# Weight sums in another order and a chunk ahead, the last gate behind the next chunk's first copy, and ScalarE and VectorE pinned to the written order in these chunks

## The chip, the core and the metric

The kernel runs on one core of a Trainium2 chip. The core has a matrix engine (TensorE), which writes its results to PSUM banks, a vector engine (VectorE), a scalar engine (ScalarE), GpSimd, and a sync engine that issues transfers. Each engine takes the instructions of its own queue one after the other and waits for the others through semaphores. The metric is the time of one execution on the device in microseconds; lower is better.

## What is computed

A stack of four layers over 256 tokens of width 1024, in float32. Each layer is a feed-forward block, an attention, and a second feed-forward block, each between norms and with a residual:

```python
def swiglu(x, w_in, w_out):
    gate, up = jnp.split(x @ w_in, 2, axis=-1)
    return (jax.nn.silu(gate) * up) @ w_out

for i in range(DEPTH):                       # DEPTH = 4
    h = h + 0.5 * rms_norm(swiglu(rms_norm(h, g[0]), ffn_w_in[i, 0], ffn_w_out[i, 0]), g[1])
    m = rms_norm(h, g[2])
    ...                                      # one of three kinds of attention
    h = h + rms_norm(m, g[3])
    h = h + 0.5 * rms_norm(swiglu(rms_norm(h, g[4]), ffn_w_in[i, 1], ffn_w_out[i, 1]), g[5])
```

The change touches the eight feed-forward blocks alone. A block's `w_in` is 1024 x 5632 (gate and up side by side), its `w_out` 2816 x 1024.

## The kernel before

**Products in three matmuls.** Every float32 weight is split into a high and a low part (`hilo`, lines 155 to 157): ScalarE copies the raw weights rounded to `hi` (line 156), VectorE subtracts `hi` from the raw ones to get `lo` (line 157). A product takes hi times hi, lo times hi and hi times lo, so three matmuls for each 128 rows of weights (`product`, line 152). A unit of weights is 128 partitions x 2048 elements, and its product on one token tile of 128 tokens is 12 matmuls of 512 columns.

**Chunks.** A block walks over the 2816 columns in six chunks: chunk 0 of 512, chunk 1 of 256, chunks 2 to 5 of 512. Chunks 0 and 1 go the plain way (`plain`). Chunks 2 to 5 (`WINO`) use a Winograd form of the 2 x 2 product of token tiles by gate and up: seven products instead of eight, of sums of the weights' four quarters. The quarters are b00 and b01 (upper half of the rows, gate and up) and b10 and b11 (lower half). Seven weight units come of them: b00, b10, t2 = b00 + b01 + b11, t1 = b00 + b01, t3 = b01 + b11, b11, and t4 = t2 + b10.

**How the sums are made before.** `plan_wino` (lines 359 to 400) splits b00, then VectorE adds b01 into b00's buffer (line 372, this is t1); it splits b10, then VectorE adds b00's buffer (now t1) and b11 into a fifth buffer, t2 (line 372 again), and GpSimd issues a transfer that adds b11 into b01's buffer (line 375, this is t3); it splits t2, then GpSimd adds b10 into t2's buffer (line 375, this is t4). So a chunk has two sums on VectorE and two accumulating transfers.

**One chunk on TensorE** (`wino`, lines 470 to 522). Bank B (tile `pb`) takes the product of b00; ScalarE copies it out as `sl0` (line 487). The gated result of the chunk before is turned (tile `tpg`, line 434) and split into `gh` and `gl`. Bank A (`pa`) takes b10; VectorE adds it to `sl0` (line 482, a small operation), ScalarE takes Silu (line 493). B takes t2 on top, and is copied out as `sl1` (line 498); then come the output products of the chunk before with its first `w_out` unit, o0, token tile 0 and then 1 (tile `y`, lines 244 to 246); B takes t1 on top and is copied out as `g1` (line 504); bank C (`pc`) takes t3, VectorE adds it to `g1` (line 482); B takes b11 on top, and VectorE makes the gated result of tile 0, `g` (`up`, line 426); output products with the second `w_out` unit, o2; C takes t4 on top. The last gate, of tile 1: VectorE adds C to `sl1` (line 482), ScalarE takes Silu (line 518), VectorE multiplies (line 426).

**What sets the order.** The code is handed to a scheduling pass, which orders each engine's queue by its own estimate of when operands are ready; the written order decides only where that pass sees a tie or a dependence. Weight units live in four buffers (`UNITS`): a split has to wait until TensorE is done with the unit that had the buffer before. Raw weights live in nine (`RAWS`). `fill` issues the next loads and splits as buffers are free.

## Time and profile before

| | |
|---|---|
| time, median of 3 runs | 2004.0 us (2003.55 to 2004.16) |
| profiled execution | 2004.23 us, of which the span of the instructions is 2002.3 us |
| TensorE busy | 1932.5 us, 97% of the span |
| VectorE busy | 1609.4 us, 80% |
| ScalarE busy | 1257.2 us, 63% |
| mean granted TensorE clock | 0.998 of full speed |

Busy time of TensorE is time in which at least one matmul is under way; matmuls overlap, so the idle time that the profile lists for it is only what is left between the end of one and the start of the next. A wait is written as the waiting instruction, an arrow, and the instruction that ended last among those it waited for.

### The profile page before, as it was taken

The page shows a single profiled execution, that of the slowest core. Times are in us where ns is not written, and L with a number is a line of the kernel's source. Part 1 is how long each engine was busy: PE and PEld are TensorE (multiplying, and loading weights), DVE is VectorE, ACT ScalarE, POOL GpSimd, SP SyncE. Part 2 cuts the span into 40 slices and gives each one's busy share as a digit, 9 for nine tenths or more (in the row PEclk, how much of TensorE's full clock was granted, in tenths as well). Part 3 has the DMA queues.
Part 4 walks back from the last instruction along what each step waited for, and adds up shares of the span by engine and source line. Part 5 has one row for each costly group of instructions (what it writes and reads, how often), then busy time and mean ns, then how long its engine had stood idle before and what let it go on. Part 6 is the DMA issues. An engine that isn't in the chain of part 4 may idle for free.

```text
span 2002.3 us, 25733 instructions
## 1 busy us (share of the span) xinstructions
PE 1932.5 (97%) x9712; PEld 1584.9 (79%) x9712; DVE 1609.4 (80%) x2040; ACT 1257.2 (63%) x1721; POOL 188.6 (9%) x303
## 2 busy tenths in 40 slices
PE   7999999999999999999999999999999999999998
PEld 6777878777877878877887787678778777878776
DVE  6888678888788766788879877877988888678886
ACT  6566666566566566566656666865666657576654
POOL 0001210000000120000000032000000000210000
PEclk9999999999999999999999999999999999999999
DMA  9795638696787556687877675166868785638782
GB/s 360 213 295 140 211 120 294 184 294 188 245 274 222 169 189 212 184 278 211 283 221 212 209 205 165 60 242 200 230 208 300 202 286 148 206 105 286 203 286 55
DMA packets 177867, 430.25 MB, mean 215 GB/s; under 512 B 8784, under 2 KB 37712, under 8 KB 169552
## 3 DMA queue, kind: packets, MB, share of 16 engines
q1 hardware_dynamic: 168528, 361.51, 50.7%
q0 software_dynamic: 9216, 67.11, 17.6%
q8 instruction: 76, 1.25, 0.2%
q14 instruction: 47, 0.39, 0.1%
HBM read 360.43 MB, written 1.05 MB: 181 GB/s over the span
## 4 chain that ended last, share of the span: by engine, by line
PE 79%; ACT 8%; DVE 7%; issue 3%; POOL 0%; ACTq 0%; DVEq 0%; POOLq 0%
PE ps L152 13%; PE pb L152 12%; PE y L246 9%; PE y L244 9%; PE y L245 9%; PE pc L152 6%; ACT hi L156 5%; PE pa L152 4%; PE pw L670 4%; PE pw L672 4%; PE pw L671 3%; DVE lo L157 3%; DVE raw L372 2%; PE tpg L434 1%; ACT gh L156 1%
## 5 line engine op out<-in xcount | busy, mean ns | idle before, releaser
L157 DVE TENSOR_TENSOR lo<-raw,hi 128x2048 fp32r<-128x2048 f32 (+3 forms) x534 | 984.7, 1861 | 251.3 <-ACT hi L156 250.8
L156 ACT CAST hi<-raw 128x2048 fp32r<-128x2048 f32 (+3 forms) x534 | 824.8, 1563 | 481.6 <-DVE raw L372 189.9
L244 PE MATMUL y<-hi,gh 128*128 128x512 f32 x704 | 277.6, 394 | 5.1 <-ACT gh L156 5.1
L245 PE MATMUL y<-lo,gh 128*128 128x512 f32 x704 | 275.2, 391 | 0.0
L246 PE MATMUL y<-hi,gl 128*128 128x512 f32 x704 | 265.7, 391 | 0.0
L152 PE MATMUL ps<-hi,xh 128*128 128x256 f32 (+1 forms) x512 | 175.4, 342 | 1.9 <-ACT xh L156 1.3
L152 PE MATMUL pb<-hi,sh 128*128 128x512 f32 x384 | 153.1, 399 | 21.1 <-ACT sl L487 21.1
L152 PE MATMUL ps<-lo,xh 128*128 128x256 f32 (+1 forms) x512 | 173.2, 338 | 0.2 <-DVE lo L157 0.2
L152 PE MATMUL ps<-hi,xl 128*128 128x256 f32 (+1 forms) x512 | 172.9, 338 | 0.0
L244 PEld LDWEIGHTS y<-hi,gh 128*128 128x128 f32 x704 | 132.2, 188 | 41.7 <-ACT gh L156 15.2
L670 PE MATMUL pw<-hi,xh 128*128 128x512 f32 (+2 forms) x432 | 164.6, 381 | 0.0
L672 PE MATMUL pw<-hi,xl 128*128 128x512 f32 (+2 forms) x432 | 155.9, 361 | 0.0
L671 PE MATMUL pw<-lo,xh 128*128 128x512 f32 (+2 forms) x432 | 155.4, 360 | 0.0
L246 PEld LDWEIGHTS y<-hi,gl 128*128 128x128 f32 x704 | 132.2, 188 | 27.4
L375 POOL DMA_DIRECT2D raw<-raw x64 | 55.5, 868 | 1037.6 <-DVE raw L372 644.3
L245 PEld LDWEIGHTS y<-lo,gh 128*128 128x128 f32 x704 | 132.3, 188 | 26.0
L152 PE MATMUL pb<-lo,sh 128*128 128x512 f32 x384 | 151.8, 395 | 0.0
L152 PE MATMUL pb<-hi,sl 128*128 128x512 f32 x384 | 149.5, 389 | 0.0
L372 DVE TENSOR_TENSOR raw<-raw,raw 128x2048 f32<-128x2048 f32 x64 | 146.0, 2282 | 0.0
L152 PEld LDWEIGHTS ps<-hi,xh 128*128 128x128 f32 x512 | 97.6, 191 | 13.2 <-ACT xh L156 2.2
L152 PEld LDWEIGHTS pb<-hi,sh 128*128 128x128 f32 x384 | 72.0, 188 | 45.3 <-ACT sl L487 31.2
L152 PEld LDWEIGHTS ps<-lo,xh 128*128 128x128 f32 x512 | 97.6, 191 | 11.2 <-DVE lo L157 1.1
(213 smaller groups left out, 3327.2 us busy)
## 6 DMA issues: line engine op xcount, KB each, us to landing
raw<-in_ffn_w_in SPq DMA_DIRECT2D x172, 1024.0 KB, 8.4
raw<-in_ffn_w_out SPq DMA_DIRECT2D x88, 1024.0 KB, 9.2
raw<-raw POOLq DMA_DIRECT2D x64, 1024.0 KB, 7.0
raw<-in_diff_w_in SPq DMA_DIRECT2D x24, 1024.0 KB, 5.2
raw<-in_moba_w_in SPq DMA_DIRECT2D x12, 1024.0 KB, 5.2
raw<-in_nsa_w_in SPq DMA_DIRECT2D x9, 1024.0 KB, 5.1
raw<-in_diff_w_out SPq DMA_DIRECT2D x8, 1024.0 KB, 4.9
gpre<-in_norm_g SPq DMA_DIRECT2D x12, 512.0 KB, 5.9
```

What stands on the lines that cost most here:

```text
L152: nc.tensor.matmul(out, l, r, start=first and i == 0, stop=last and i == len(steps) - 1, skip_group_check=more)
L156: self.nc.scalar.copy(hi, src)
L157: self.nc.vector.tensor_tensor(lo, src, hi.bitcast(F32), op=ALU.subtract)
L244: nc.tensor.matmul(y[b], x[0][:, kt, :], hi[:, k, s], start=f, stop=False)
L245: nc.tensor.matmul(y[b], x[0][:, kt, :], lo[:, k, s], start=False, stop=False)
L246: nc.tensor.matmul(y[b], x[1][:, kt, :], hi[:, k, s], start=False, stop=l)
L372: nc.vector.tensor_tensor(R[name(to)], R[name(a)], R[name(b)], op=ALU.add)
L375: nc.gpsimd.dma_start(R[name(to)], R[name(b)], accum_op=ALU.add)
L434: nc.tensor.transpose(tp[:, k, :], g[:, k * P:(k + 1) * P], self.ident)
L670: nc.tensor.matmul(out, x[0][:, kt, :], hi[:, k, :], start=first and i == 0, stop=False)
L671: nc.tensor.matmul(out, x[0][:, kt, :], lo[:, k, :], start=False, stop=False)
L672: nc.tensor.matmul(out, x[1][:, kt, :], hi[:, k, :], start=False, stop=last and i == len(todo) - 1)
```

## The change

Three things change in the Winograd chunks, none in the arithmetic of a product.

- **Sums.** A new `sums_of(j)` makes t1 = b00 + b01 on VectorE into the fifth buffer, and has GpSimd add b11 into b01 (t3). It is called one chunk ahead: in chunk j - 1 between the output products with o0 and the product of t1, and for chunk 2 in the plain chunk 1. When chunk j's units are prepared, b00 and b10 are split, and VectorE adds b01, which by then holds t3, into b00: that is t2. So the second sum now reads what the first transfer has written. After the split of t2, GpSimd adds b10 into b00's buffer (t4).
- **Last gate.** The three instructions of tile 1's last gate become `gate1`, which the next chunk calls right behind its copy of `sl0`; the last one is called after the loop.
- **Order.** While `wino` runs, `ordered` is set, and every split, copy, Silu, sum and small operation on ScalarE and VectorE that goes through `placed` is tied behind the instruction written before it on its engine. The scheduling pass no longer moves them.

The diff, cut to its core:

```diff
     def hilo(self, src, hi, lo):
-        self.nc.scalar.copy(hi, src)
-        self.nc.vector.tensor_tensor(lo, src, hi.bitcast(F32), op=ALU.subtract)
+        self.placed(self.nc.scalar.copy(hi, src))
+        self.placed(self.nc.vector.tensor_tensor(lo, src, hi.bitcast(F32), op=ALU.subtract))
+
+    def placed(self, ins):
+
+        return self.tc.keep_in_program_order(ins) if self.ordered else ins
...
-                               (name("b10"), quarter(1, 0)), (name("b11"), quarter(1, 1)), (name("t2"), None), *ko):
+                for n, src in ((name("b00"), quarter(0, 0)), (name("b01"), quarter(0, 1)), (name("b11"), quarter(1, 1)),
+                               (name("t1"), None), (name("b10"), quarter(1, 0)), *ko):
...
+                def sum_t2():
+                    split(name("b10"), name("b10"))
+                    self.placed(nc.vector.tensor_tensor(R[name("b00")], R[name("b00")], R[name("b01")], op=ALU.add))
+
+                def split_t2():
+                    split(name("t2"), name("b00"))
+                    nc.gpsimd.dma_start(R[name("b00")], R[name("b10")], accum_op=ALU.add)
...
-                    lambda: quarters("b00", [("b00", "b00", "b01")]),
-                    lambda: quarters("b10", [("t2", "b00", "b11"), ("b01", "b11")]),
-                    lambda: quarters("t2", [("t2", "b10")]),
+                    lambda: split(name("b00"), name("b00")),
+                    sum_t2,
+                    split_t2,
...
+            def sums_of(j):
...
+                while (j, "t1") not in R:
+                    loads.pop(0)()
+                b01 = R[j, "b01"]
+                self.placed(nc.vector.tensor_tensor(R[j, "t1"], R[j, "b00"], b01, op=ALU.add))
+                nc.gpsimd.dma_start(b01, R[j, "b11"], accum_op=ALU.add)
...
-            def wino(j):
+            def wino(j, gate1):
...
-                nc.scalar.copy(sl0, B)
+                place(nc.scalar.copy(sl0, B))
+                gate1()
...
                 o(1, 0)
+                sums_of(j + 1)
                 times(B, s31, 4, "t1", False)
...
-                add(sl1, C)
-                nc.scalar.activation(sl1, sl1, AF.Silu, scale=X[1][1])
-                up(1, g1, 512, sl1, j, nr[1], g1)
-                fill()
+
+                def gate1():
+                    add(sl1, C)
+                    place(nc.scalar.activation(sl1, sl1, AF.Silu, scale=X[1][1]))
+                    up(1, g1, 512, sl1, j, nr[1], g1)
...
-                    wino(j)
+                    self.ordered = True
+                    gate1 = wino(j, gate1)
+                    self.ordered = False
...
-                plain(j, zig, [lambda: turn(j - 1, 0), lambda: turn(j - 1, 1)])
+                plain(j, zig, [lambda: turn(j - 1, 0), lambda: turn(j - 1, 1), lambda: sums_of(j + 1)])
```

What it does to the queues is shown at the seam from chunk 3 to chunk 4 of layer 0's second block. Names: `pb`, `pa`, `pc` are the banks, `g01_3_1` the gated result of chunk 3, tile 1.

VectorE before. lo439 is o2 of chunk 2, lo441 t4 of chunk 3, lo445, lo446 and lo447 are b00, b10 and t2 of chunk 4, lo448 is o0 of chunk 3; raw423, raw424 and raw433 are b00, b01 and b11 of chunk 4, raw436 its t2:

```order
L157 TENSOR_TENSOR lo439_3537<-raw421_3320,hi439_3536 128x2048
L482 TENSOR_TENSOR g01_3_1_3554<-pc444_3564,g01_3_1_3554 128x512
L157 TENSOR_TENSOR lo441_3557<-raw416_3266,hi441_3556 128x2048
L157 TENSOR_TENSOR lo445_3579<-raw423_3350,hi445_3578 128x2048
L426 SCALAR_TENSOR_TENSOR g01_3_0_3595<-pb431_3433,st396_3004,sl01_3_0_3446 128x512
L372 TENSOR_TENSOR raw423_3350<-raw423_3350,raw424_3352 128x2048
L157 TENSOR_TENSOR lo446_3598<-raw430_3431,hi446_3597 128x2048
L372 TENSOR_TENSOR raw436_3482<-raw423_3350,raw433_3452 128x2048
L482 TENSOR_TENSOR sl01_3_1_3504<-pc444_3564,sl01_3_1_3504 128x512
L157 TENSOR_TENSOR lo447_3628<-raw436_3482,hi447_3627 128x2048
L426 SCALAR_TENSOR_TENSOR g01_3_1_3554<-g01_3_1_3554,st397_3006,sl01_3_1_3504 128x512
L157 TENSOR_TENSOR lo448_3648<-raw438_3510,hi448_3647 128x2048
```

VectorE after, the same stretch; raw433 is now t1 of chunk 4, lo449 is o0 of chunk 3:

```order
L158 TENSOR_TENSOR lo439_3537<-raw421_3320,hi439_3536 128x2048
L411 TENSOR_TENSOR raw433_3452<-raw423_3350,raw424_3352 128x2048
L158 TENSOR_TENSOR lo441_3559<-raw395_2990,hi441_3558 128x2048
L497 TENSOR_TENSOR g01_3_1_3556<-pc444_3566,g01_3_1_3556 128x512
L158 TENSOR_TENSOR lo445_3581<-raw423_3350,hi445_3580 128x2048
L439 SCALAR_TENSOR_TENSOR g01_3_0_3596<-pb429_3424,st396_3004,sl01_3_0_3437 128x512
L158 TENSOR_TENSOR lo446_3599<-raw436_3481,hi446_3598 128x2048
L379 TENSOR_TENSOR raw423_3350<-raw423_3350,raw424_3352 128x2048
L158 TENSOR_TENSOR lo447_3628<-raw423_3350,hi447_3627 128x2048
L497 TENSOR_TENSOR sl01_3_1_3504<-pc444_3566,sl01_3_1_3504 128x512
L439 SCALAR_TENSOR_TENSOR g01_3_1_3556<-g01_3_1_3556,st397_3006,sl01_3_1_3504 128x512
L158 TENSOR_TENSOR lo449_3663<-raw438_3510,hi449_3662 128x2048
```

The first sum moved five places forward, behind lo of o2; the small operation on `sl01_3_1` moved from ahead of lo of t2 to behind it, with the multiplication (`g01_3_1`) directly after it.

ScalarE before, from the split of t2 on; hi448 is o0 of chunk 3, hi451, hi454 and hi456 are t1, t3 and b11 of chunk 4:

```order
L156 CAST hi447_3627<-raw436_3482 128x2048
L518 ACTIVATE sl01_3_1_3504<-sl01_3_1_3504,st368_2826 128x512
L156 CAST hi448_3647<-raw438_3510 128x2048
L487 COPY sl01_4_0_3666<-pb450_3653 128x512
L156 CAST hi451_3668<-raw423_3350 128x2048
L156 CAST gh01_3_0_3679<-tpg01_3_0_3674 128x512
L156 CAST hi454_3698<-raw424_3352 128x2048
L156 CAST gh01_3_1_3708<-tpg01_3_1_3703 128x512
L498 COPY sl01_4_1_3724<-pb450_3653 128x512
L156 CAST hi456_3726<-raw433_3452 128x2048
L493 ACTIVATE sl01_4_0_3666<-sl01_4_0_3666,st350_2752 128x512
```

ScalarE after; hi449 is o0:

```order
L157 CAST hi447_3627<-raw423_3350 128x2048
L502 COPY sl01_4_0_3657<-pb448_3644 128x512
L537 ACTIVATE sl01_3_1_3504<-sl01_3_1_3504,st368_2826 128x512
L157 CAST hi449_3662<-raw438_3510 128x2048
L157 CAST hi451_3668<-raw433_3452 128x2048
L157 CAST gh01_3_0_3678<-tpg01_3_0_3673 128x512
L509 ACTIVATE sl01_4_0_3657<-sl01_4_0_3657,st350_2752 128x512
L157 CAST hi454_3697<-raw424_3352 128x2048
L157 CAST gh01_3_1_3708<-tpg01_3_1_3703 128x512
L514 COPY sl01_4_1_3724<-pb448_3644 128x512
L157 CAST hi456_3726<-raw431_3446 128x2048
```

The copy of bank B (`sl01_4_0`) moved ahead of the last gate's Silu and of the split of o0; the Silu of tile 0 moved from behind the split of b11 to ahead of the split of t3.

TensorE before, at the output products of the same chunk; `y409` is token tile 0, `y410` tile 1:

```order
L152 MATMUL pb450_3653<-hi447_3627,sl01_0_2997 128x512
L244 MATMUL y409_0_0_3184<-hi448_3647,gh01_3_0_3679 128x512
L245 MATMUL y409_0_0_3184<-lo448_3648,gh01_3_0_3679 128x512
L244 MATMUL y409_0_1_3185<-hi448_3647,gh01_3_0_3679 128x512
L245 MATMUL y409_0_1_3185<-lo448_3648,gh01_3_0_3679 128x512
L244 MATMUL y410_1_0_3210<-hi448_3647,gh01_3_1_3708 128x512
```

TensorE after, from the end of the first output product on:

```order
L251 MATMUL y409_0_1_3185<-hi449_3662,gl01_3_0_3679 128x512
L153 MATMUL pc463_3786<-hi454_3697,sh01_1_3000 128x512
L249 MATMUL y410_1_0_3210<-hi449_3662,gh01_3_1_3708 128x512
L250 MATMUL y410_1_0_3210<-lo449_3663,gh01_3_1_3708 128x512
L249 MATMUL y410_1_1_3211<-hi449_3662,gh01_3_1_3708 128x512
L250 MATMUL y410_1_1_3211<-lo449_3663,gh01_3_1_3708 128x512
L153 MATMUL pb448_3644<-hi451_3668,sh01_1_3000 128x512
```

Before, tile 1's product begins after four matmuls of tile 0's. After, all twelve of tile 0's and the first matmul of t3 (`pc`) stand ahead of it, and behind its first four stand seven matmuls of t1 (`pb`) and then its other eight.

## Rows read from the trace of the kernel before

**Rows 1.** Page, part 1: engine, busy us, share of the span, instructions.

```profile
PE 1932.5 (97%) x9712; PEld 1584.9 (79%) x9712; DVE 1609.4 (80%) x2040; ACT 1257.2 (63%) x1721; POOL 188.6 (9%) x303
```

**Rows 2.** Waits of TensorE: engine, tile, line, releaser, total us, times, longest us.

```profile
PE pb L152 <- ACT sl L487: 21.1, 24, 0.9
PE tpg L434 <- DVE g L426: 14.1, 8, 1.8
PE y L244 <- ACT gh L156: 5.1, 24, 0.2
```

**Rows 3.** Timeline, VectorE, one chunk: start us, duration us, instruction, idle before it.

```profile
421.10 2.28 DVE L372 TENSOR_TENSOR raw<-raw,raw 128x2048 f32<-128x2048 f32 x1
...
425.42 2.29 DVE L157 TENSOR_TENSOR lo<-raw,hi 128x2048 fp32r<-128x2048 f32 x1 [1.44 <-ACT hi L156]
427.63 0.75 DVE L426 SCALAR_TENSOR_TENSOR g<-g,st,sl 128x512 f32<-128x512 f32 x1
...
432.70 0.68 DVE L157 TENSOR_TENSOR gl<-tpg,gh 128x512 fp32r<-128x512 f32 x1
433.30 0.68 DVE L482 TENSOR_TENSOR sl<-pa,sl 128x512 f32<-128x512 f32 x1
...
441.41 2.29 DVE L157 TENSOR_TENSOR lo<-raw,hi 128x2048 fp32r<-128x2048 f32 x1 [2.44 <-ACT hi L156]
...
453.68 2.28 DVE L372 TENSOR_TENSOR raw<-raw,raw 128x2048 f32<-128x2048 f32 x1
```

**Rows 4.** Timeline, ScalarE, the same chunk.

```profile
423.49 1.90 ACT L156 CAST hi<-raw 128x2048 fp32r<-128x2048 f32 x1 [8.16 <-DVE raw L372]
425.30 0.72 ACT L518 ACTIVATE sl<-sl,st 128x512 f32<-128x512 f32 x1
425.92 1.89 ACT L156 CAST hi<-raw 128x2048 fp32r<-128x2048 f32 x1
427.71 0.57 ACT L487 COPY sl<-pb 128x512 f32<-128x512 f32 x1
...
432.27 0.60 ACT L156 CAST gh<-tpg 128x512 fp32r<-128x512 f32 x1
...
439.46 1.91 ACT L156 CAST hi<-raw 128x2048 fp32r<-128x2048 f32 x1 [3.67 <-issue]
```

**Rows 5.** Timeline, TensorE, the seams from chunk 2 to chunk 5.

```profile
373.27 0.39 PE L244 MATMUL y<-hi,gh 128*128 128x512 f32 x1
...
375.99 0.39 PE L152 MATMUL pb<-hi,sh 128*128 128x512 f32 x1
...
391.55 0.55 PE L434 MATMUL tpg<-ident,g 128*128 128x128 f32 x3 [1.76 <-DVE g L426]
...
428.34 0.51 PE L152 MATMUL pb<-hi,sh 128*128 128x512 f32 x1 [0.90 <-ACT sl L487]
...
432.93 0.50 PE L244 MATMUL y<-hi,gh 128*128 128x512 f32 x1 [0.21 <-ACT gh L156]
...
438.99 0.39 PE L246 MATMUL y<-hi,gl 128*128 128x512 f32 x1
...
465.51 0.50 PE L244 MATMUL y<-hi,gh 128*128 128x512 f32 x1 [0.21 <-ACT gh L156]
```

**Rows 6.** GpSimd's accumulating transfers: one issue; all landings; issues from 427.5 to 437.

```profile
428.07 0.85 POOL L375 DMA_DIRECT2D raw<-raw  x1 [7.89 <-DVE lo L157]
...
DMA to landing us min/median/max: 6.9/7.0/9.7
...
raw<-in_ffn_w_in SPq DMA_DIRECT2D x2, 1024.0 KB, 9.0
raw<-raw POOLq DMA_DIRECT2D x1, 1024.0 KB, 8.1
```

**Rows 7.** Timeline, chunk 2: VectorE's small operation on sl0 and ScalarE's Silu.

```profile
369.82 0.68 DVE L482 TENSOR_TENSOR sl<-pa,sl 128x512 f32<-128x512 f32 x1
...
370.54 0.73 ACT L493 ACTIVATE sl<-sl,st 128x512 f32<-128x512 f32 x1 [0.27 <-DVE sl L482]
```

More of the change, by code (lines that the diff above doesn't have):

```diff
@@ L410, in unit @@
             def unit(n):
[L411 removed]
+                if n not in U:
+                    fill()
                 return U[n]
@@ L497, in wino @@
                 sl1 = tile("sl", 1)
-                nc.scalar.copy(sl1, B)
+                place(nc.scalar.copy(sl1, B))
                 fill()
```

42 lines of the change are left out of this document (20 added, 22 removed).

## Prediction

> **What bounds the kernel now.** I read the page first: TensorE is busy for 97% of the span, VectorE for 80% [rows 1], so time can only be won where TensorE waits. The list of TensorE's waits names them [rows 2]: `pb` waits for ScalarE's copy out of its bank (line 487) 24 times, 21.1 us; a transpose `tpg` waits for VectorE's gate 8 times, 14.1 us; the output product waits for `gh` 24 times, 5.1 us. 8 and 24 are one and three for each of the eight feed-forward blocks: all sit at the seams between Winograd chunks. Then I read one seam, chunk 3 to chunk 4 of the second block, engine by engine.
>
> On VectorE [rows 3], the two sums of a chunk stand in its busiest stretch; the second starts at 421.10 here and at 453.68 one chunk later, so a chunk takes 32.58 us. On ScalarE [rows 4], the split of t2 can start only when that sum is done (423.49, after 8.16 us idle); the Silu and a split come next, and only then (427.71) the copy that TensorE wants. TensorE [rows 5] starts t2 at 428.34 after 0.90 us of idle time and is stopped once more at 432.93, for `gh`. Both stops together are under 1.5 us of 32.58; the rest is TensorE's own work. VectorE waits 1.44 us and 2.44 us in such a chunk [rows 3], both times for a split on ScalarE. So VectorE works 28.7 us of the 32.58. That is the number to keep in mind: it has 3.9 us to give before it sets the pace itself.
>
> **What the change removes.** If the order did nothing but good, the copy would come right behind the split of t2 and all three waits of rows 2 could go: 40.3 us.
>
> **What the written order adds.** No instruction is added or taken away, and the number of large VectorE passes per chunk is the same (nine splits, two sums). What changes is who stands behind whom. By the pieces of order in the change's section, VectorE now has lo of t2 ahead of the two small operations of the last gate, where the first used to fill the wait for the split of t2 and the second came after it. ScalarE has the gate's Silu ahead of the o0 split, and the Silu of token tile 0 ahead of the t3 split. Each pair is a hand-over to the other engine and back, with the engine's whole queue behind it. I walk one chunk, in us from the start of the second sum. Durations are those of rows 3 and 4: sum or lo 2.28, small operation 0.68, up 0.75, split 1.90, Silu 0.72, `gh` 0.60; an instruction that waits for nothing starts 0.08 (VectorE) or 0.10 (ScalarE) before the end of the one before; hand-overs cost 0.11 from VectorE to ScalarE (423.38 to 423.49), 0.03 back (425.39 to 425.42), 0.06 from ScalarE to TensorE (432.87 to 432.93) and 0.08 from TensorE to ScalarE (439.38 to 439.46, [rows 4, 5]).
>
> - Sum until 2.28; split of t2 from 2.39 to 4.29; lo of t2 from 4.32. VectorE has waited 2.1.
> - Small operation on sl1 from 6.52 to 7.20; Silu from 7.31 to 8.03; up from 8.06. Waited 0.9.
> - Split of o0 behind that Silu, from 7.93 to 9.83; lo of o0 from 9.86. Waited 1.1. Then lo of t1 from 12.06, `gl` of tile 0 at 14.26, small operation on sl0 from 14.86 to 15.54.
> - Silu of tile 0 from 15.65; split of t3 from 16.27 to 18.17; lo of t3 from 18.20. Waited 2.7, with ScalarE's queue behind the Silu: `gh` of tile 1 ends only at 18.67, and TensorE begins the second output product at 18.73.
> - From there to the last matmul of o0 are 19 matmuls (8 and 4 of the product, 7 of t1 that the order puts between). At 0.2267 each (12 from 373.27 to 375.99, [rows 5]) the last one starts at 22.81 and ends at 23.20. The o2 split needs o0's buffer, so it runs from 23.28 to 25.18, and lo of o2 starts at 25.21. VectorE was done at 23.2: waited 2.0.
> - Then without a wait: the early sum 27.41, lo of t4 29.61, small operation 31.81, lo of b00 32.41, up 34.61, lo of b10 35.28, and the next second sum at 37.48.
>
> So VectorE closes a ring of 37.48 us instead of 32.58: its own work is as before, and five waits of 8.9 us stand where there were 3.9.
>
> **The accumulate moves onto that ring.** The second sum now reads b01 after GpSimd's accumulate into it. The early sum ends at 29.69; GpSimd issues 0.36 later (VectorE's end at 427.71, issue at 428.07, [rows 3, 6]), at 30.05. Landing takes 6.9 to 9.7 us, in the middle 7.0 [rows 6]. With 6.9 it is there at 36.95, half a microsecond ahead of the sum; with the 8.1 of the accumulate that had weight loads issued beside it [rows 6], at 38.15. In the new order the buffer that lo of o2 frees and the one that lo of t4 frees both start a load around this accumulate, so I take 8.1: a chunk of 38.15. In the old order nobody needed this accumulate soon.
>
> **The first seam, chunk 2 to 3.** Chunk 2's Silu of tile 0 now stands ahead of the t3 split, as in the ScalarE piece of order. The small operation before it is at 369.82, the Silu at 370.54 as today [rows 7]; the t3 split then starts at 371.17 and ends at 373.07. TensorE needs it at 373.27 [rows 5], so this alone costs nothing. But six matmuls of t1 (seven in later chunks) and one of t3 now stand ahead of the end of the second output product, where today t1 begins behind it, at 375.99 [rows 5]: it ends at 377.8 instead of 376.2, the t4 split waits for its buffer until 377.8, lo of t4 starts at 379.8, the early sum of chunk 3 at 382.0, ending 384.25. GpSimd issues at 384.6; with 7.0 (no load is issued near it) the second sum starts at 391.6, up at 393.8, ending 394.54, and the transpose at 394.6 instead of 391.55 [rows 5]: 3.05 later.
>
> **The sum.** The second sum of chunk 3 at 391.6, of chunk 4 at 391.6 + 38.15 = 429.75, of chunk 5 at 467.9. TensorE's second output product of that seam starts 18.73 later, at 486.63, against 465.51 [rows 5]. By then it has done nine matmuls more than today (eight of the first output product, one of t3): 2.04 us. Behind this point the chunk has only TensorE's own products left. So a block ends 486.63 - 465.51 - 2.04 = 19.1 us later, eight blocks 153 us. The profiled execution took 2004.2 us (span 2002.3 and 1.9 around it), the median of the three runs is 2004.0: they are the same, and the forecast is **2157 us**. With the accumulate always in time (37.48, 391.6) a block gives 17.7 us and the whole 2146; that is the low end of the mechanism.
>
> **Rivals.**
> - *The waits are hidden and the stops go.* If VectorE's hand-overs found slack as they do today, TensorE would lose only the waits of rows 2: 2004.2 - 40.3 = **1964 us**, faster. For it: VectorE is idle 20% of the span. Against it: 3.9 us of idle time per chunk, and the walk needs 8.9. It decides the sign at 3.9 us of waits per chunk. The Trainium skill (Perfetto Trace Analysis, section Identifying the Most-Contended Engine) says to optimise the engine with the highest occupancy and fill its gaps; read over the whole span that points at TensorE and at this rival. The chunk's rows speak against that reading here.
> - *The accumulate is slower still.* With 9.7 us, the largest landing [rows 6], the period is 39.75 and the first seam 2.7 later: a block 25.0 us later, **2204 us**. For it: up to two loads beside it. Against it: one of 64 took as long.
> - *The order is the same in effect.* If the pins held nothing that the planner had not chosen, the time would stay at 2004. The listed order is different, so I give it little.
>
> **How the numbers follow.** Forecast with its own range (2146 to 2157 and some us per seam for what the walk rounds): 0.82. Slow accumulate: 0.11. Hidden waits: 0.05. No effect: 0.02. The range 2130 to 2190 holds the forecast and the nearer half of the slow accumulate; the low end is two us per block under 2146, for waits that overlap more than I let them. Within 0.2% counts as the same, which is about what runs of this kernel can tell: faster 0.05, same 0.02, slower 0.93.
>
> **What would show it.** In the profile of the changed kernel: second sums (line 379) about 38 us apart; five waits of VectorE for ScalarE in each chunk of 2.1, 0.9, 1.1, 2.7 and 2.0 us; TensorE's wait at line 487's copy gone from the list, and in its place waits of the output product for `gh` and `gl` (about 2.6 and 1.9 us) and of `pc` for the t3 split (about 1.4 us), 24 times each; the transpose's wait longer than 1.8 us; ScalarE waiting for the small VectorE operations. If the second sum waits for a transfer by more than 1 us, the slow accumulate is right. If sums are 32 us apart or less, the forecast is wrong in its main step, and the waits of ScalarE at the two Silus would be the place to look.

## The result, and the profile after

The changed kernel takes 2190.35 us, the median of four runs (2186.22 to 2192.33), against 2004.08 us before (2003.55 to 2004.86): the ratio is 1.093, with a 95% interval of 1.0907 to 1.0945. The forecast was 2157 us with a range of 2130 to 2190, so the sign and the mechanism came out, and the size lies on the upper edge of the range (the median 0.35 us beyond it, the profiled execution within), 33 us above the likeliest value. The profiled execution took 2186.22 us, its span is 2184.5.

The first part of the page, as in [rows 1] (engine, busy us, share of the span, instructions):

```profile
PE 2011.2 (92%) x9712; PEld 1627.0 (74%) x9712; DVE 1618.3 (74%) x2040; ACT 1257.6 (58%) x1721; POOL 188.7 (9%) x303
```

No engine has more instructions than before. VectorE and ScalarE work as long as before to within 9 us, and the share of each is lower: all engines wait more. TensorE is busy 79 us longer for the same number of matmuls; its granted clock is 0.964 in this execution, 0.998 before (more below).

The waits of TensorE, as in [rows 2] (engine, tile, line, releaser, total us, times, longest us):

```profile
PE y L249 <- ACT gh L157: 40.0, 24, 2.2
PE pb L153 <- DVE lo L158: 36.9, 24, 2.1
PE y L251 <- DVE gl L158: 34.7, 25, 1.7
PE tpg L448 <- DVE g L439: 19.4, 8, 3.5
...
PE pb L153 <- ACT sl L502: 6.9, 6, 1.8
PE pc L153 <- ACT hi L157: 5.8, 6, 1.1
```

The wait at the copy of `sl0`, 21.1 us in [rows 2], is down to 6.9: the copy comes sooner, as the change has it. In its place stand waits for `gh`, `gl` and lo of t2, once per seam (24 or 25 times each).

VectorE, the same chunk as in [rows 3], from the second sum of chunk 4 to that of chunk 5 in the second block (start us, duration us, instruction, idle before it and its releaser):

```profile
459.49 2.29 DVE L379 TENSOR_TENSOR raw<-raw,raw 128x2048 f32<-128x2048 f32 x1 [2.00 <-DMA raw<-raw]
463.83 2.29 DVE L158 TENSOR_TENSOR lo<-raw,hi 128x2048 fp32r<-128x2048 f32 x1 [2.05 <-ACT hi L157]
...
467.51 0.75 DVE L439 SCALAR_TENSOR_TENSOR g<-g,st,sl 128x512 f32<-128x512 f32 x1 [0.79 <-ACT sl L537]
469.30 4.50 DVE L158 TENSOR_TENSOR lo<-raw,hi 128x2048 fp32r<-128x2048 f32 x2 [1.04 <-ACT hi L157]
...
474.31 0.68 DVE L497 TENSOR_TENSOR sl<-pa,sl 128x512 f32<-128x512 f32 x1
477.57 2.29 DVE L158 TENSOR_TENSOR lo<-raw,hi 128x2048 fp32r<-128x2048 f32 x1 [2.58 <-ACT hi L157]
...
484.73 2.29 DVE L158 TENSOR_TENSOR lo<-raw,hi 128x2048 fp32r<-128x2048 f32 x1 [2.06 <-ACT hi L157]
486.93 2.29 DVE L411 TENSOR_TENSOR raw<-raw,raw 128x2048 f32<-128x2048 f32 x1
489.13 2.29 DVE L158 TENSOR_TENSOR lo<-raw,hi 128x2048 fp32r<-128x2048 f32 x1
...
494.80 2.28 DVE L158 TENSOR_TENSOR lo<-raw,hi 128x2048 fp32r<-128x2048 f32 x1
499.83 2.29 DVE L379 TENSOR_TENSOR raw<-raw,raw 128x2048 f32<-128x2048 f32 x1 [2.74 <-DMA raw<-raw]
```

Read the brackets from the top: five waits for ScalarE of 2.05, 0.79, 1.04, 2.58 and 2.06 us, which the forecast put at 2.1, 0.9, 1.1, 2.7 and 2.0. Then, after lo of b10, VectorE stands idle for another 2.74 us before the second sum, and the releaser there is no engine but the accumulating transfer. The chunk takes 499.83 - 459.49 = 40.34 us; 32.58 before. The five waits are the same in all eight blocks to within 0.1 us, with two exceptions: the last is longer in some (below), and from chunk 3 to 4 the first is 1.4 us. The wait for the transfer is not the same everywhere, and this chunk is one of the slower ones. Over the run it is this line, of which 8.7 us belong to chunk 2 of the first block:

```profile
DVE raw L379 <- DMA raw<-raw: 54.6, 25, 8.7
```

The other 45.9 us are 2.4 to 4.8 us for the second sum of chunk 3, 0.6 to 2.4 us (median 0.8) for that of chunk 4 and 0.7 to 3.0 us (median 1.5) for that of chunk 5, in every block.

ScalarE at the longest of the five waits, to be read with [rows 4]:

```profile
475.03 0.72 ACT L509 ACTIVATE sl<-sl,st 128x512 f32<-128x512 f32 x1 [3.48 <-DVE sl L497]
475.66 1.88 ACT L157 CAST hi<-raw 128x2048 fp32r<-128x2048 f32 x1
477.44 0.58 ACT L157 CAST gh<-tpg 128x512 fp32r<-128x512 f32 x1
```

The Silu of tile 0 waits 3.48 us for VectorE's small operation (474.31), and behind it in ScalarE's queue stand the split of t3, for which VectorE then waits, and `gh` of tile 1, for which TensorE waits. In [rows 4] `gh` stood at 432.27, 11.2 us after the second sum; now it stands 17.95 us after it.

TensorE, the same chunk, as in [rows 5]:

```profile
464.33 0.50 PE L153 MATMUL pb<-hi,sh 128*128 128x512 f32 x1 [0.79 <-ACT sl L502]
466.18 0.50 PE L153 MATMUL pb<-lo,sh 128*128 128x512 f32 x1 [1.34 <-DVE lo L158]
...
471.60 0.50 PE L249 MATMUL y<-hi,gh 128*128 128x512 f32 x1 [0.59 <-ACT gh L157]
...
474.45 1.22 PE L251 MATMUL y<-hi,gl 128*128 128x512 f32 x2 [1.65 <-DVE gl L158]
475.47 0.63 PE L249 MATMUL y<-hi,gh 128*128 128x512 f32 x1
475.90 0.63 PE L250 MATMUL y<-lo,gh 128*128 128x512 f32 x1
```

It is stopped four times, and behind the fourth stop the matmuls start 0.43 us apart (475.47, 475.90) instead of 0.23. That is about half the rate, the lower of the clock's two levels. The window of this chunk says the same; its columns are the length, the busy us of each engine with its instructions, the granted clock, the DMA share and GB/s:

```profile
459.49:499.83 40.34, 35.97 (x145) 28.11 (x144) 29.08 (x19) 20.39 (x16) 1.71 (x2) 0.92 0.69 212
```

TensorE is "busy" for 35.97 us here mainly because some of its matmuls are slower, with a granted clock of 0.92; VectorE's own work, 29.08 us, is close to the 28.7 of before.

### The profile page after: what moved, and what is told of

It reads as the page before. It is cut to its first block, busy times and chain, and to the rows that moved or that the text cites. A ratio compares the mean times of both kernels' runs of the same rounds, so it can differ in the third digit from the quotient of the medians.

```text
span 2184.5 us, 25682 instructions
## 1 busy us (share of the span) xinstructions
PE 2011.2 (92%) x9712; PEld 1627.0 (74%) x9712; DVE 1618.3 (74%) x2040; ACT 1257.6 (58%) x1721; POOL 188.7 (9%) x303
## 4 chain that ended last, share of the span: by engine, by line
PE 33%; issue 15%; DVE 9%; DMA 9%; ACT 5%; POOL 0%; POOLq 0%; DVEq 0%; ACTq 0%; SPq 0%
DMA raw<-raw 6%; PE ps L153 5%; DVE lo L158 5%; PE y L251 4%; PE y L249 4%; PE y L250 4%; ACT hi L157 4%; PE pb L153 3%; PE pw L694 2%; DMA raw<-in_ffn_w_in 2%; PE pw L696 2%; PE pw L695 2%; PE pc L153 2%; DVE raw L379 2%; PE sc L768 1%
## 5 line engine op out<-in xcount | busy, mean ns | idle before, releaser
L249 PE MATMUL y<-hi,gh 128*128 128x512 f32 x704 | 293.8, 419 | 40.0 <-ACT gh L157 40.0
L251 PE MATMUL y<-hi,gl 128*128 128x512 f32 x704 | 283.5, 420 | 34.7 <-DVE gl L158 34.7
L250 PE MATMUL y<-lo,gh 128*128 128x512 f32 x704 | 289.7, 412 | 0.0
L249 PEld LDWEIGHTS y<-hi,gh 128*128 128x128 f32 x704 | 140.8, 200 | 80.5 <-ACT gh L157 50.8
L251 PEld LDWEIGHTS y<-hi,gl 128*128 128x128 f32 x704 | 138.7, 202 | 77.1 <-DVE gl L158 49.7
L250 PEld LDWEIGHTS y<-lo,gh 128*128 128x128 f32 x704 | 141.0, 200 | 30.5 <-DVE lo L158 2.3
L379 DVE TENSOR_TENSOR raw<-raw,raw 128x2048 f32<-128x2048 f32 x32 | 73.3, 2290 | 54.6 <-DMA raw<-raw 54.6
L153 PEld LDWEIGHTS ps<-lo,xh 128*128 128x128 f32 x512 | 97.6, 191 | 11.2 <-DVE lo L158 1.0
L153 PEld LDWEIGHTS ps<-hi,xl 128*128 128x128 f32 x512 | 97.5, 190 | 11.1 <-DVE xl L158 1.1
L153 PEld LDWEIGHTS pb<-lo,sh 128*128 128x128 f32 x384 | 73.8, 192 | 42.6 <-DVE lo L158 27.4
```

The source lines that it names most:

```text
L153: nc.tensor.matmul(out, l, r, start=first and i == 0, stop=last and i == len(steps) - 1, skip_group_check=more)
L249: nc.tensor.matmul(y[b], x[0][:, kt, :], hi[:, k, s], start=f, stop=False)
L250: nc.tensor.matmul(y[b], x[0][:, kt, :], lo[:, k, s], start=False, stop=False)
L251: nc.tensor.matmul(y[b], x[1][:, kt, :], hi[:, k, s], start=False, stop=l)
L379: self.placed(nc.vector.tensor_tensor(R[name("b00")], R[name("b00")], R[name("b01")], op=ALU.add))
```

## The experiments

Three explanations stood against each other. **Ring:** the written order hands work from VectorE to ScalarE and back with the whole queue behind it, so VectorE needs longer for a chunk than TensorE. **Transfer:** the second sum now waits for an accumulating transfer of 7 to 10 us, and the order matters little. **Clock:** TensorE runs at half rate behind its stops.

A number that comes up in most runs is the chunk, from one second sum to the next, worked out from the starts of that sum's line in the eight blocks. The first column contains a shift of chunk 2's sum against TensorE's work, so the others say more.

| kernel | time, us | chunk 2 to 3 | 3 to 4 | 4 to 5 (medians, us) |
|---|---|---|---|---|
| before | 2004 | 33.2 | 32.6 | 32.6 |
| changed | 2190 | 41.5 | 38.7 | 39.8 |
| order alone | 2135 | 34.2 | 37.8 | 37.8 |
| sums alone | 2023 | 40.8 | 31.6 | 32.3 |
| early sum sooner | 2124 | 41.8 | 35.5 | 35.4 |
| Silu 0 behind t3 | 2135 | 40.7 | 36.2 | 38.0 |
| small operation ahead of lo of t2 | 2123 | 41.4 | 36.3 | 37.5 |
| all three | 2016 | 39.9 | 32.0 | 32.5 |
| turns first | 1971 | 36.7 | 30.3 | 30.3 |
| early sum sooner, no ties | 1979 | 37.1 | 30.5 | 30.4 |

### The parts of the change, one at a time

**Sums alone.** Against the changed kernel, the last gate goes back to its place and nothing is tied:

```diff
-        return self.tc.keep_in_program_order(ins) if self.ordered else ins
+        return ins
...
-                gate1()
                 fill()
                 turn(j - 1, 0)
...
+                add(sl1, C)
+                place(nc.scalar.activation(sl1, sl1, AF.Silu, scale=X[1][1]))
+                up(1, g1, 512, sl1, j, nr[1], g1)
+                fill()
```

> The weight sums of the changed kernel alone: the last gate stands where it stood before, and nothing is tied to the written order. Ring theory (the time is lost because the written order hands VectorE and ScalarE work to each other with the whole queue behind it): the sums cost nothing by themselves. Without ties the small operations can go back into the waits, VectorE's waits for ScalarE are near the 3.9 us of a chunk before, and the chunks 4 and 5 follow at about 32 us. What is left is the transfer ahead of chunk 3's second sum, which comes late because chunk 2's early sum does: one stop of 4 us in a block. The stops of before (6.2 us a block) would be mostly gone, so 1975 to 2005 us. Accumulate theory (the time is lost because the second sum now waits for a transfer of 7 to 10 us): that wait is kept here, so the time stays above 2100 us. Clock theory (the time is lost because TensorE runs at 1.2 GHz behind its stops): follows the stops, so it gives the ring's number here.

(The order of the loads, which belongs to the sums, stays as in the changed kernel.) Measured: 2022.99 us, ratio 1.0094 (1.0077 to 1.0111). That is far from the 2100 of the transfer explanation, and it misses the ring's range too: slower than before, not faster. VectorE and TensorE of this kernel at chunk 3 show why. First VectorE:

```profile
397.74 2.29 DVE L379 TENSOR_TENSOR raw<-raw,raw 128x2048 f32<-128x2048 f32 x1 [4.15 <-DMA raw<-raw]
```

and TensorE:

```profile
402.07 0.62 PE L153 MATMUL pb<-hi,sh 128*128 128x512 f32 x1 [3.18 <-ACT hi L157]
404.40 0.80 PE L153 MATMUL pb<-lo,sh 128*128 128x512 f32 x1 [1.71 <-DVE lo L158]
```

The second sum of chunk 3 waits 4.15 us for the transfer, and TensorE stops twice for t2, 4.9 us in all. The line of the early sums' transfers in this kernel says how long they took:

```profile
DMA to landing us min/median/max: 7.6/11.0/12.2
```

Before it was 6.9, 7.0 and 9.7 [rows 6]. So the sums do have a price, 19 us, and it is paid at the first seam: the second sum of chunk 3 waits 2.5 to 4.9 us for its transfer in every block, 26 us together, and the eight first seams are 25 us longer than before. It is not the length of the transfer alone. Those of chunk 3 took 8.1 us in the middle; those of chunks 4 and 5 took 11.2 and 11.7, and yet these chunks, at 31.6 and 32.3 us, have no loss. Chunk 3's early sum, and with it the transfer, comes too late.

**Order alone.** The kernel before, with the ties:

```diff
-        self.nc.scalar.copy(hi, src)
-        self.nc.vector.tensor_tensor(lo, src, hi.bitcast(F32), op=ALU.subtract)
+        self.placed(self.nc.scalar.copy(hi, src))
+        self.placed(self.nc.vector.tensor_tensor(lo, src, hi.bitcast(F32), op=ALU.subtract))
...
-                    wino(j)
+                    self.ordered = True
+                    wino(j)
+                    self.ordered = False
```

(and the same for the copies, Silus, sums and small operations).

> The kernel before with the ties to the written order alone: sums, transfers and last gate as before. Ring theory: slower by most of the loss, since the hand-overs of the written order are there and no transfer is on the ring: walking the written order with the durations of before gives a chunk of 37.7 us instead of 32.6 and 25 us of stops in a block, against 10 us by the same walk for the order of before, so 2004 + 8 x 15 = about 2125 us (2100 to 2160). Accumulate theory: no change, 2004 us, since nothing waits for a transfer. Clock theory: as the ring, but the granted clock would have to be as low as in the changed kernel (0.964) for the same time.

Measured: 2134.79 us, ratio 1.0651 (1.0636 to 1.0667). VectorE from a second sum on:

```profile
443.76 2.28 DVE L377 TENSOR_TENSOR raw<-raw,raw 128x2048 f32<-128x2048 f32 x1
448.09 2.29 DVE L158 TENSOR_TENSOR lo<-raw,hi 128x2048 fp32r<-128x2048 f32 x1 [2.05 <-ACT hi L157]
...
451.77 0.75 DVE L431 SCALAR_TENSOR_TENSOR g<-g,st,sl 128x512 f32<-128x512 f32 x1 [0.79 <-ACT sl L525]
453.56 4.57 DVE L158 TENSOR_TENSOR lo<-raw,hi 128x2048 fp32r<-128x2048 f32 x2 [1.04 <-ACT hi L157]
...
461.92 2.29 DVE L158 TENSOR_TENSOR lo<-raw,hi 128x2048 fp32r<-128x2048 f32 x1 [2.59 <-ACT hi L157]
...
469.09 2.29 DVE L158 TENSOR_TENSOR lo<-raw,hi 128x2048 fp32r<-128x2048 f32 x1 [2.08 <-ACT hi L157]
```

These are the same five waits, with the old sums, and no second sum of this kernel waits for a transfer. The chunk is 37.8 us, VectorE's ring by itself. The larger part of the loss, 131 of 186 us, is the order.

**Last gate alone**, and **sums and gate without ties:**

```diff
                 nc.scalar.copy(sl0, B)
+                gate1()
```

> The move of the last gate alone, nothing tied, old sums. Without ties the scheduling pass puts the gate's small operation and Silu where its own estimate wants them: the Silu moves behind the copy of sl0, but the split of o0 stays ahead of that copy. Ring theory: VectorE keeps its slack, the copy comes at the same time or up to 0.7 us earlier (a Silu of 0.72 us less ahead of it), so 1990 to 2004 us. Rival (the gate's move is what makes VectorE wait): above 2040 us.

```diff
-        return self.tc.keep_in_program_order(ins) if self.ordered else ins
+        return ins
```

> The changed kernel whole, sums and gate moved, but nothing tied to the written order. Ring theory: as the sums alone, 1975 to 2005 us; so the whole loss of 186 us, and more, hangs on the ties. If sums and gate together do harm that neither does alone: clearly above the run with the sums alone.

Measured: 2003.02 us for the gate alone, ratio 0.9996 (0.9986 to 1.0005), no change; 2024.04 us for sums and gate, ratio 1.0101 (1.0086 to 1.0116), the same as the sums alone. The place of the last gate is worth nothing when the scheduling pass may order. The parts don't add up: 131 for the order and 20 for the sums and gate make 151, and all together cost 186. The waits for the transfer close the gap. In the changed kernel the second sums wait 45.9 us for it (above), on top of the 131 of the order, which has no such wait; that makes 177 of the 182 us between the profiled executions. In the sums alone the wait costs only at the first seam, and their chunks from 3 to 4 and 4 to 5 give 9 us back, which the ring doesn't.

### One hand-over at a time, all ties kept

Each of these three takes the changed kernel and moves one step in the written order.

**The early sum sooner:**

```diff
                 o(0, 0)
-                o(1, 0)
                 sums_of(j + 1)
+                o(1, 0)
```

> The changed kernel, all ties kept, with one call moved: the early sum stands ahead of the second output product instead of behind it, so on VectorE ahead of lo of o2 instead of behind it. Ring theory with the transfer on it: the sum of 2.2 us falls into VectorE's wait of 2.0 us for the split of o2, and the transfer is issued some 4.4 us earlier in the chunk, so that it lands before the second sum wants it. The chunk goes from the measured 39.2 to 35.3 (VectorE alone) or 35.8 us (a landing of 10 us): 3.5 to 4 us less at three seams of eight blocks, 2190 - 84 to 96 = 2095 to 2105 us. If the transfer isn't on the ring: only the wait of 2.0 us goes, 2190 - 48 = 2142 us. If the hand-overs play no part and only the transfer does: below 2060 us.

Measured: 2123.82 us, ratio 1.0600 (1.0579 to 1.0621). VectorE from sum to sum:

```profile
444.27 2.28 DVE L379 TENSOR_TENSOR raw<-raw,raw 128x2048 f32<-128x2048 f32 x1
...
467.35 2.29 DVE L411 TENSOR_TENSOR raw<-raw,raw 128x2048 f32<-128x2048 f32 x1
469.55 4.55 DVE L158 TENSOR_TENSOR lo<-raw,hi 128x2048 fp32r<-128x2048 f32 x2
...
479.68 2.28 DVE L379 TENSOR_TENSOR raw<-raw,raw 128x2048 f32<-128x2048 f32 x1
```

The early sum (467.35) fills the wait for the split of o2: lo of o2 and of t4 (469.55) now start without one. The second sum (479.68) waits for nothing. The chunk is 35.4 us, 35.3 was expected. (By the lists in the change's section the first sum had moved forward by four places, not five; this is one call more.) The total missed its number of 2095 to 2105, since only two seams of a block gained: at the first one the transfer is issued sooner but lands after up to 12.2 us, and the median from chunk 2 to 3 stays at 41.8.

**Silu of tile 0 behind the split of t3**, and **the small operation ahead of lo of t2:**

```diff
                 add(sl0, A)
-                place(nc.scalar.activation(sl0, sl0, AF.Silu, scale=X[0][1]))
                 fill()
                 turn(j - 1, 1)
+                place(nc.scalar.activation(sl0, sl0, AF.Silu, scale=X[0][1]))
```

> The changed kernel, all ties kept, with one instruction moved: the Silu of token tile 0 stands behind the split of t3 and gh of tile 1 on ScalarE instead of ahead of them; VectorE's small operation on sl0 stays where it is. Ring theory: the split of t3 no longer waits for VectorE and back, so VectorE's wait of 2.7 us there goes, and with it TensorE's stop of 2.2 us for gh. The chunk is 2.7 us shorter, at three seams of eight blocks: 2190 - 65 = 2125 us (2110 to 2140). If this hand-over were hidden by the wait for the transfer: above 2175 us. If all hand-overs but this one were harmless: near 2020 us.

```diff
-                while preps and live["unit"] < UNITS:
+                while preps and live["unit"] < UNITS and not (held and getattr(preps[0], "__name__", "") == "split_t2"):
...
+                held.append(1)
                 if j < last and chunks[j - 1][1] == 512:
...
                 times(C, X[1][0], 4, "t4", False)
+                add(sl1, C)
+                held.clear()
+                fill()
 
                 def gate1():
-                    add(sl1, C)
```

> The changed kernel, all ties kept, with the small operation of the last gate put back ahead of lo of t2 on VectorE (the split of t2 is held until it is written; Silu and multiplication stay behind the copy of sl0). Ring theory: the small operation fills 0.6 us of the 2.1 us in which VectorE waits for the split of t2, the Silu is done by the end of lo of t2 (wait of 0.9 gone), and the split of o0 starts 2.6 us earlier (wait of 1.1 gone): the chunk is 2.6 us shorter, 2190 - 62 = 2128 us (2110 to 2145). If hidden by the wait for the transfer: above 2175 us.

Measured: 2135.33 us, ratio 1.0658 (1.0636 to 1.0679), and 2123.37 us, ratio 1.0598 (1.0577 to 1.0619). Expected were 2125 and 2128. Each of these two hand-overs, taken out, is worth what the ring says it is worth, to within some 10 us, and each shows in the chunk from 3 to 4: 38.7 to 36.2 and to 36.3.

**All three** edits together:

> The three moves of the runs before together, all ties kept. Ring theory: VectorE's chunk would be 37.5 - 2.0 - 2.7 - 2.6 = 30.2 us, less than TensorE's own 31.2, so that TensorE sets the pace again and most of its 6 us of stops per block before are gone: 1955 to 1985 us, faster than the kernel before though every instruction is tied as in the changed one. If tying costs something by itself, or the sums in the new order can't work: above 2004 us. Between them, 1985 to 2004: the transfer still stops the second sum, as in the run with the sums alone, where it landed after up to 12 us.

Measured: 2015.99 us, ratio 1.0061 (1.0044 to 1.0077). The ring is gone, with 32.0 and 32.5 us for a chunk, and 174 of the 186 us came back with every tie in place. The same sums and gate without any tie took 2024 us, so tying costs nothing by itself here; which order is tied does. But the expectation of 1955 to 1985 us is missed, and the time isn't below before. What is late now is at the first seam, on VectorE:

```profile
392.56 2.29 DVE L379 TENSOR_TENSOR raw<-raw,raw 128x2048 f32<-128x2048 f32 x1 [4.46 <-DMA raw<-raw]
394.77 0.74 DVE L441 SCALAR_TENSOR_TENSOR g<-pb,st,sl 128x512 f32<-128x512 f32 x1
```

and TensorE:

```profile
395.57 0.69 PE L450 MATMUL tpg<-ident,g 128*128 128x128 f32 x2 [4.11 <-DVE g L441]
```

The second sum waits 4.46 us for its transfer, the gate of tile 0 stands behind the sum, and TensorE waits 4.11 us for the gate. The transfers of the early sums in this kernel:

```profile
DMA to landing us min/median/max: 8.1/11.3/12.5
```

### A version that beats both

The waits that were left named the next moves: issue the transfer sooner, and let nothing that TensorE wants soon stand behind the sum that waits for it.

```diff
+                turn(j - 1, 1)
                 add(sl0, A)
-                place(nc.scalar.activation(sl0, sl0, AF.Silu, scale=X[0][1]))
                 fill()
-                turn(j - 1, 1)
+                sums_of(j + 1)
                 times(B, s24, 0, "t2", False)
                 sl1 = tile("sl", 1)
+                place(nc.scalar.activation(sl0, sl0, AF.Silu, scale=X[0][1]))
                 place(nc.scalar.copy(sl1, B))
...
+                held.add("sum_t2")
                 g1 = tile("g", 1)
...
                 up(0, B, 512, sl0, j, nr[0])
+                held.remove("sum_t2")
+                held.add("split_t2")
```

(beside the edits for the small operation on sl1; `held` now names the step ahead of which the preparing of units stops.)

> The run with all three moves, with three more of the same kind, all ties kept: the early sum stands ahead of the product of t2 (its transfer is issued some 8 us sooner), the second sum waits until the gate of token tile 0 is written (so that the transposes of that gate don't stand behind the transfer), and gh of both token tiles is written ahead of the splits of t1 and t3. Ring theory with the transfer on it: the run before lost its gain at the transfer (10 to 12 us beside the loads) ahead of chunk 3's gate, 4.3 us a block; with 8 us more of lead a landing of 12 us is in time, and TensorE is stopped for 2 to 3 us a block instead of the 6.2 of the kernel before: 1955 to 1985 us, faster than before. If the loads bunch further and land too late for their splits: 1985 to 2030 us, with stops of VectorE or ScalarE for loads.

Measured: 1970.94 us, ratio 0.9835 (0.9819 to 0.9852), faster than both. The transfers still take 8.1 to 12.5 us (median 11.2), but little waits for them. VectorE's line, of which 8.0 us are once more chunk 2 of the first block:

```profile
DVE raw L379 <- DMA raw<-raw: 15.5, 10, 8.0
```

Of the 24 second sums of chunks 3 to 5, 15 don't wait, and nine wait 0.2 to 1.7 us, 7.5 us together. TensorE's waits in the chunks:

```profile
PE pb L153 <- ACT sl L504: 9.5, 8, 2.7
...
PE tpg L450 <- DVE g L441: 2.3, 4, 0.8
...
PE y L251 <- DVE gl L158: 1.9, 7, 0.3
```

13.7 us in all, 40.3 in [rows 2]; and the window of a chunk, from 400.00 to 430.60, in the columns as above:

```profile
400.00:430.60 30.60, 30.60 (x141) 25.34 (x140) 29.21 (x20) 20.91 (x17) 1.71 (x2) 1.00 0.91 281
```

TensorE is busy for all of 30.60 us at the full clock, with VectorE at 29.21. The same early sum without any tie:

```diff
                 fill()
+                sums_of(j + 1)
                 turn(j - 1, 1)
...
                 o(1, 0)
-                sums_of(j + 1)
```

> The sums alone without ties, as in the first run of the study (2023 us), with the early sum moved ahead of the product of t2. If what made that run slower than the kernel before is the transfer that landed after 8 to 12 us, its lead of some 10 us more hides it: 1955 to 1990 us. If it was slower because of the sums themselves or the loads: 2000 us or above.

Measured: 1979.03 us, ratio 0.9873 (0.9858 to 0.9888). Against the sums alone this is 44 us less for one line moved, and no second sum of chunk 3 waits for its transfer any more. That shows what made the sums cost 19 us: the time between the early sum and the second sum was too short for the transfer.

### The clock, and the sum without a transfer

**Products of zeros** in TensorE's stop:

```diff
+                def still(t, n):
+                    hi = unit((j - 1, "o", 0))[0]
+                    for _ in range(n):
+                        nc.tensor.matmul(y[t][0], self.zero, hi[:, 0, 0:512], start=False, stop=False)
+                still(0, 2)
                 o(0, 0)
+                still(1, 6)
                 o(1, 0)
```

> The changed kernel with eight more products in each Winograd chunk, of a zero matrix into the banks of the output products, so that nothing changes in the result: they stand where TensorE waits for gh of token tile 0 and are there to shorten its stop, so that it finds the granted clock higher when it goes on. In the changed kernel about 50 us of matmul time are added by matmuls at half rate right behind such stops. Clock theory (that time is part of the loss): 2190 - 20 to 50 = 2140 to 2170 us, if the clock stays up. Ring theory (VectorE sets the pace, so TensorE's slower matmuls are covered): no gain; where the stop is shorter than eight matmuls, they push the second half of a chunk back, 24 x 0.25 = 6 us, so 2190 to 2200 us. If the granted clock doesn't rise, the run tells only the price of eight matmuls.

Measured: 2184.30 us (2182.69 to 2193.90), ratio 1.0909 (1.0885 to 1.0933); the interval overlaps that of the changed kernel. The clock did rise:

```profile
core 0: 2181.0 us, clock 0.984
```

It was 0.964 over 2184.5 us, so the time lost to the lower level, worked out from the two shares, went from 79 to 35 us, and the kernel hardly got faster. The clock theory's 20 to 50 us aren't there. They are not quite zero either: the changed kernel shows chunks in which the half rate lasts longer, and then VectorE's wait for the split of o2 (2.06 us above) is longer too, as here in the fifth block:

```profile
1216.65 2.29 DVE L158 TENSOR_TENSOR lo<-raw,hi 128x2048 fp32r<-128x2048 f32 x1 [3.36 <-ACT hi L157]
```

The split of o2 wants o0's buffer, which TensorE's slower matmuls release later. Over the 16 chunks 3 and 4 this wait exceeds 2.03 us by 6.8 us together. With the products of zeros it is 2.0 to 2.1 us in all 16. That is the size of the difference of the two medians, 6 us, which the intervals alone can't tell from none. The traces don't settle it either: with the zeros the second sum of chunk 5 waits 18.4 us for its transfer over the eight blocks, 13.2 without, and the 16 chunks together are only 2.8 us shorter.

**t3 on VectorE** instead of by transfer, in the kernel with the sums alone:

```diff
-                nc.gpsimd.dma_start(b01, R[j, "b11"], accum_op=ALU.add)
+                self.placed(nc.vector.tensor_tensor(b01, b01, R[j, "b11"], op=ALU.add))
```

> The sums alone without ties, as in the first run of the study (2023 us), with the sum t3 = b01 + b11 on VectorE instead of a transfer by GpSimd: 2.3 us more of VectorE's work in each chunk, and no transfer ahead of the second sum. If the transfer is what made the sums cost 19 us: that goes, and what VectorE's 2.3 us cost at the first seam comes in its place, 2000 to 2010 us. If the sums cost it in another way: 2023 us or more, since VectorE has more to do.

Measured: 2015.32 us, ratio 1.0058 (1.0042 to 1.0075): less than 2023, more than the 2010 expected. From chunk 3 on, its seams take the same time as before to within 0.1 us (one of 24 excepted, 0.7); what it costs is 1.4 us at each first seam, 11 us in eight blocks. VectorE's 2.3 us stand there ahead of two things that TensorE waits for, a lo (no such wait in the list of before) and the gate (14.1 us before):

```profile
PE tpg L448 <- DVE g L439: 16.2, 8, 2.0
...
PE pb L153 <- DVE lo L158: 4.1, 8, 0.5
```

These two are 6 us more than before. Other waits at the seams are 4 us shorter, and TensorE is busy 9 us longer (1941.2 us), so how the 11 us come together is not shown.

## Why the prediction was right, and what it had wrong

**What bounds the kernel.** Right. 3.9 us of VectorE's slack in a chunk decided the sign; order alone (37.8 us a chunk, five waits) shows it without the rest of the change.

**The walk.** Right to 0.12 us where it can be compared on VectorE: from the second sum on, the forecast put lo of t3 at 18.20, lo of o2 at 25.21, the early sum at 27.41, lo of t4 at 29.61 and lo of b10 at 35.28; the trace has 18.08, 25.24, 27.44, 29.64 and 35.31 (starts above, less 459.49).

**The terms of the sum.** Over eight blocks, from the trace (first seam: from the small operation on sl0 in chunk 2 to the second sum of chunk 3; tail: from the second sum of chunk 5 to that operation in the next block, or to the end):

| term | forecast, us | measured, us |
|---|---|---|
| ahead of the first block's small operation | 0 | 1.7 |
| first seam, 8 x 3.05 | 24.4 | 31.9 |
| chunk 3 to 4, 8 x 5.57 | 44.6 | 51.1 |
| chunk 4 to 5, 8 x 5.57 | 44.6 | 58.0 |
| tail, 8 x 4.86 | 38.9 | 39.6 |
| together | 152.5 | 182.3 |

**The step that was mis-sized** is "so I take 8.1" for the accumulate's landing, and 7.0 at the first seam. The line of the early sums' transfers in the changed kernel:

```profile
DMA to landing us min/median/max: 6.9/8.2/12.4
```

By chunk, the medians from issue to landing are 7.0 us for chunk 3, 8.2 for chunk 4 and 8.9 for chunk 5. The forecast is right for chunk 4. For chunk 5 (up to 10.4 us) two or three loads were issued or under way beside the transfer in every block, but so were two for chunk 4, so their number doesn't tell the two apart. At the first seam three blocks of eight had 7.6 to 9.1 us instead of 6.9 or 7.0 (their first seams are 4.2 to 5.8 us later, the other five 3.4 to 3.6). Why chunk 5 and these three blocks were slower stays open; the slowest of the three, 9.1 us, had next to no load beside it. Of the 27 us by which the three terms with a transfer in them are short, the longer landings are some 15 (11 at the two later chunks, 4 at the first seam) and the longer waits for the split of o2, which go with the clock, 6.8. The other 5 or so are mostly 0.3 to 0.5 us at each first seam and have no cause here. The prediction's own sign for it was there: "if the second sum waits for a transfer by more than 1 us, the slow accumulate is right"; it does so in 15 of 24 seams, 2.0 and 2.7 us in the rows above. The truth lies between the forecast and that rival, which I had given 0.11 and the largest landing of before as its price; landing times of a kernel whose transfers are in nobody's way were a poor bound for one where loads start beside them. That the measured time lies on the edge of the range, and not well beyond it, is in part luck: the upper part of the range had been made for this rival, not for the forecast.

**The list of waits.** Right in kind for `gh` (mostly 2.2 us, 0.59 in the chunk shown, about 2.6 forecast), for `gl` (1.65 here, about 1.9 forecast), for the longer wait of the transpose and for ScalarE at its Silus. The wait at the copy was to be gone, and 6 of 24 are left. Wrong for `pc`: 6 waits instead of 24. TensorE came later than the walk had it, with matmuls 0.43 us apart behind the stop for `gl`; the six waits are at those stops behind which it kept its rate. And one wait was not on the list, for lo of t2 (36.9 us): a later second sum stops TensorE there. The places of TensorE's stops were forecast worse than their sum, as one expects where another engine sets the pace.

**The rivals.** That the waits would hide is excluded by order alone, and that the order is the same in effect by the same run. That the time lies in who stands behind whom, and not in added work, is what the all-three run shows: 174 us came back by moving three steps. What the prediction did not say is that the sums cost something without the ties, too (19 us), through the same transfer.

The Trainium skill (Perfetto Trace Analysis, section Identifying the Most-Contended Engine) would have the engine of highest occupancy optimised first, and judges TensorE's headroom by the share of its peak that it reaches and by the busy share of its weight loads, not of its matmuls. By matmuls that engine is TensorE before and after (97% and 92%), as the prediction read it; by weight loads it is level with VectorE (79% against 80% before, 74% against 74% after). The one run that edited TensorE's own queue, with products of zeros, gained nothing that can be told from no change; the gains came from the order on VectorE and ScalarE, at 74% and 58% after.

## What to carry to other kernels

Before you tie instructions to the written order, write down one turn of the loop for each engine that has only a few microseconds of slack, with every hand-over to another engine and back: each costs the other engine's whole instruction, and a small operation put behind a large one carries its waiters along. A tie is as good as the order that it holds, so mend the pairs before untying all: here the kernel with the ties was 186 us slower than before in one order and 33 us faster in another (25 us of that came without any tie, too, from the early sum alone). Where an instruction is moved behind a transfer, give that transfer the landing time that it has beside loads, not the one it has alone, and issue it as soon as its operands are there.

## What the runs showed of the hardware that I had not expected

An accumulating transfer of 1 MB from SBUF to SBUF takes longer where more weight loads are under way beside it. For each of the 64 transfers of a kernel I added up the time in which weight loads ran beside it and divided by its own time:

| loads beside it, on the mean | before: count, median us | all three: count, median us | turns first: count, median us |
|---|---|---|---|
| under 0.5 | 40, 6.9 | 8, 7.0 | 11, 7.1 |
| 0.5 to 1 | 16, 8.0 | 20, 8.1 | 18, 8.1 |
| 1 to 1.5 | 8, 8.2 | 11, 8.2 | 11, 8.3 |
| 1.5 and more | none | 25, 11.5 | 24, 11.4 |

The loads were not varied by themselves, so this goes with them and is not shown to come from them. Nor is it the whole: in the changed kernel no transfer had 1.5 loads or more beside it, and single ones still took 11 to 12.4 us, one of 9.1 us with next to none. In the kernel before no transfer had 1.5 loads or more beside it either, so its trace could not have shown the last row. The DMA share of a chunk was 0.69 in the changed kernel and 0.91 in the fastest one, but 0.85 before, where transfers took 7.0 us in the middle, so the share alone doesn't tell how long they take.

In the changed kernel TensorE's clock fell to its lower level behind many of its stops in the chunks, stops of 0.8 to 3.5 us, for up to 13 matmuls in a row that started 0.43 us apart instead of 0.23. There were about 250 such matmuls, 50 us more than at the full clock; in the kernel before none in the chunks. It did not fall behind every stop: behind those of 1.00, 1.65 and 1.03 us between 432 and 439 us (second block) the matmuls kept their rate, and before, with stops of up to 1.8 us at the same seams, the granted clock was 1.00 in each of the second block's chunks. What decides between them stays open. Nearly all of the slower matmuls was covered by the wait for VectorE, as the run with the products of zeros shows: the granted clock went from 0.964 to 0.984 there, and the median time fell by 6 us.
